# A hybrid decoder block: the order of the quarter products in the input projection, the queue of its stores, and single extra matmuls

## Chip, core and metric

The kernel runs on one core of one Trainium2 chip. The time is the device time of one execution in microseconds (us), lower is better; the time before is the median of three runs.

## What is computed

One decoder layer in fp32, with 512 tokens (S), a model width of 2048 (D), 8 heads of 128, and an MLP of 8192. Cut to what matters:

```
h = rmsnorm(x, g_mix);  z = h @ w_in          # 2048 columns in, 10248 out
cb, cc, cv, q, k, v, f, gate_c, gate_a = split(z)
conv   = (cb * causal_conv3(cc * cv)) @ w_conv_out
attn   = softmax(q k^T / sqrt(128) + decay(f), causal) v @ w_attn_out
x      = x + (sigmoid(gate_c + b) * conv + sigmoid(gate_a + b) * attn) @ w_mix_out
h = rmsnorm(x, g_mlp);  x = x + (relu(h @ w_ff1) ** 2) @ w_ff2
out = rmsnorm(x, g_final)
```

The first product is called the input projection, h @ w_ff1 is ff1.

## The kernel before

Each large fp32 operand is split into a high and a low part (`split`, L99: ScalarE copies the high part, L100, VectorE subtracts it from the source, L101), and three matmuls, high x high, high x low and low x high, replace one. In `mm_cols` (L126) a weight quarter of 8 tiles stands still and the tokens move, 256 columns at a time: L139 and L141 are the matmuls with the high part, 32 in a run, L143 the 16 with the low part. `mm_rows` (L145; L156, L157 and L159) exchanges the two operands, for the attention values.

The input projection and ff1 save one product in eight by a scheme of seven products (a form of Strassen's), written as a `Group` (L168). A group covers a pair of column blocks and all tokens. Its weights are four quarters X00, X10, X01, X11, each a load of about 1 MB through SP's queue (`load`, L177, the DMA at L183) into one of four buffers x0 to x3, which a list named `free` hands out in the order in which `done` (L219) gives them back. A `run` (L189) splits one quarter, or a difference of quarters, into one of two buffers `th` and `tl`, and makes 48 matmuls with one of seven prepared token matrices: A11, A12, A22, S1, S2, S3, S4 (`Quarters`, L336, for the input projection, `Blocks`, L694, for ff1).

- `head` (L222) loads X00 and X10, runs A11 into bank a and A12 into bank b; their sum is the quarter (0,0) of the output.
- `tail` (L238) loads X01 and X11 and makes the runs S4 (bank c), S2 (bank a, on top of A11), S3 (bank d), S1 (bank a again) and A22 (bank d again). Its operands are X11, then X01 - X00, X11 - X01 and X11 - (X01 - X00) by three subtractions of VectorE ahead of S2 (`sub`, L103, the instruction at L104), and one more for A22. `snap` (L197, the copy at L200) takes a bank into an output buffer of ScalarE's, `plus` (L207) adds a bank to one by VectorE, and `put` stores the quarter. There are five output buffers (`otile`, L70).

In the input projection five groups, gV0 and four of keys and queries, are begun by their heads while the token matrices of the differences are being made (L462), and their tails follow (L466). gV0 and the key groups' quarters are not kept in between, so their tails load all four again, in the order X00, X10, X01, X11. Then come, each with head and tail together (`whole`, L457), the second value group gV1, six conv groups (L591), with attention (`attend`, L529) interleaved in the first four and the convolution (`conv_job`, L566) after, and eight groups of the gates (L606). ff1 has sixteen groups: the heads of the first two are begun together, then their tails, then the rest (L917 to the loop after it). Their `put` squares the quarters and forms sums of them in a buffer r, which GpSimd's queue stores (L852, L853).

The results of the projection go to HBM and are read again: keys, queries and values (L437, L444), conv inputs (L595), gates (L611), attention outputs (L563) and conv outputs (L579). All these stores stand in SP's queue, between the loads. GpSimd's queue holds, in this part of the kernel, memsets for attention's masks and two columns of `u` in each convolution (L571), which wait for a free buffer.

Nobody writes an order between engines by hand: the framework sorts each engine's instructions by its own model of the time, with the program's order as priority, and puts the waits.

`apart` (L581) gives some groups two extra matmuls in the run of S4, ahead of the third and the sixth of its eight tiles: 256 columns each, into a bank named spare that nobody reads. They are given to one conv group, to every third group of the gates and to every fourth of ff1. The PSUM banks p0 to p7 are laid out in the order in which the program first names them.

Of the kernel before, what the change touches and what calls it, by code (L numbers as in the profile page):

```python
# [15 lines left out]
P = 128  # L16
# [4 lines left out]
HS = S // 2  # L21
# [8 lines left out]
COL_K, COL_Q = 3 * CW + AW, 3 * CW  # L30
# [15 lines left out]
def tile_hybrid_block(ctx: ExitStack, tc, x, g_mix, w_in, b_f, b_gate, conv_w, w_conv_out,  # L46
# [74 lines left out]
    parts([P, 4, S])  # L121
    for i in range(7):
        pair(i, F32, "lay")


    def mm_cols(ps, Sx, hi, lo, first, extra=None):  # L126


        ps = ps[0].rearrange("p (j s) -> p j s", j=2)
        nq = hi.shape[1]  # L130
        for part in range(2):
            for q in range(nq):
                Sh, Sl = Sx(q)
                if extra and part == 0:
                    extra(q, Sh, hi[:, q, :])
                for j in range(2):
                    o, js = ps[:, j, :], slice(j * P, (j + 1) * P)
                    if part == 0:
                        nc.tensor.matmul(o, hi[:, q, js], Sh, start=first and q == 0 and j == 0, stop=False,  # L139
                                         skip_group_check=True)  # L140
                        nc.tensor.matmul(o, hi[:, q, js], Sl, start=False, stop=False, skip_group_check=True)  # L141
                    else:
                        nc.tensor.matmul(o, lo[:, q, js], Sh, start=False, stop=q == nq - 1, skip_group_check=True)  # L143
# [24 lines left out]
    class Group:  # L168
# [53 lines left out]
        def head(self, keep=False, between=lambda: None):  # L222
# [12 lines left out]
                self.done(1, 0)  # L235
            self.put(0, 0, s1)

        def tail(self):  # L238
            if self.at:
                X = self.X  # L240
            else:
                X = {(i, 0): self.load(i, 0) for i in range(2)}
            X[0, 1], X[1, 1] = self.load(0, 1), self.load(1, 1)
            a = self.a
            c = self.acc("c")
            self.run(c, "S4", X[1, 1], True)
# [12 lines left out]
            d1 = self.snap(d, self.scale)  # L259
            self.run(a, "S1", X[0, 0], False)  # L260
            self.done(0, 0)
            s4 = self.snap(a, self.scale)
            add(d1, d1, s4)
            self.put(1, 1, d1)
            self.plus(s4, c, self.scale)
            self.put(0, 1, s4)
            self.run(d, "A22", X[1, 0], False)
            self.done(1, 0)
            self.plus(s2, d)
            self.put(1, 0, s2)  # L270
# [162 lines left out]
    def store_v(c0, w):  # L433
        def put(i, j, v):
            c = c0 + j * w
            n = min(w, AW - c)
            nc.sync.dma_start(out=v_d[2 * i:2 * i + 2, :, c:c + n].rearrange("t p c -> p t c"), in_=v[:, :, :n])  # L437
            if n < w:
                add(fl[:, 2 * i:2 * i + 2, :], v[:, :, n:], bf.unsqueeze(1).to_broadcast([P, 2, NH]))
        return put  # L440

    def store_kq(hp):
        def put(i, j, v):
            nc.sync.dma_start(out=kq_d[j, 2 * hp:2 * hp + 2, :, i * HS:(i + 1) * HS].rearrange("b p c -> p b c"), in_=v)  # L444
        return put

    cV = COL_AV + AW // 2
# [1 line left out]
    gV0 = Group(w_in, COL_AV, COL_AV + VW, VW, Q1.moving, mm_rows, ((4,), (3,), (6,), (7,)), store_v(0, VW))  # L449

    def kq(hp, banks):
        return Group(w_in, COL_K + hp * HS, COL_Q + hp * HS, HS, Q1.moving, mm_cols, banks, store_kq(hp), QSCALE)

    def steady(n):
        return ((2 + n % 2,), (3 - n % 2,), (0,), (1,))

    def whole(g):  # L457
        g.head(True)
        g.tail()

    heads = [gV0] + [kq(hp, ((a,), (3,), (6,), (7,))) for hp, a in enumerate((0, 1, 2, 5))]
    for g in heads:  # L462
# [1 line left out]
    Q1.sums()  # L464
    ph.close()
    for g in heads:  # L466
        g.tail()
    whole(gV1)

    ph = ExitStack()  # L470
# [58 lines left out]
    def attend(h):  # L529
        kT, qT = at("kT"), at("qT")  # L530
        nc.sync.dma_start(out=kT, in_=kq_d[0, h])
        nc.sync.dma_start(out=qT, in_=kq_d[1, h])
        vv = at("vv", [P, NT, P])
        nc.sync.dma_start(out=vv, in_=v_d[:, :, h * P:(h + 1) * P].rearrange("t p c -> p t c"))
        o = bank(4, "o")
        for qi in range(NT):
            n = (qi + 1) * P
            qs = slice(qi * P, n)
            sc = bank(5 + 2 * (qi % 2), "sc")
            nc.tensor.matmul(sc[:, :n], qT[:, qs], kT[:, :n], start=True, stop=False)  # L540
# [12 lines left out]
            nc.vector.tensor_scalar(out=p[:, :n], in0=p[:, :n], scalar1=rs, scalar2=None, op0=ALU.mult)  # L553
            tp = bank(6, "tp")
            for ki in range(qi + 1):
                nc.tensor.transpose(tp[:, ki * P:(ki + 1) * P], p[:, ki * P:(ki + 1) * P], ident)
            pt = at("pt")
            nc.vector.tensor_copy(pt[:, :n], tp[:, :n])
            for ki in range(qi + 1):
                nc.tensor.matmul(o[:, qs], vv[:, ki, :], pt[:, ki * P:(ki + 1) * P], start=(ki == 0), stop=(ki == qi))  # L560
        ov = at("ov")
        nc.scalar.activation(out=ov, in_=o, func=AF.Copy)
        nc.sync.dma_start(out=a_d[h], in_=ov)  # L563


    def conv_job(f):  # L566
        cv, cc, cb = at("cv"), at("cc"), at("cb")
        for k, t in enumerate((cb, cc, cv)):
            nc.sync.dma_start(out=t, in_=z_d[k, f])
        u = at("u", [P, S + 2])  # L570
        nc.gpsimd.memset(u[:, 0:2], 0.0)  # L571
        nc.vector.tensor_tensor(out=u[:, 2:], in0=cv, in1=cc, op=ALU.mult)
        w = [cwT[:, i * CT + f:i * CT + f + 1] for i in range(3)]
        y = at("y")
        nc.vector.tensor_scalar(out=y, in0=u[:, 0:S], scalar1=w[0], scalar2=None, op0=ALU.mult)
        for i in (1, 2):
            nc.vector.scalar_tensor_tensor(out=y, in0=u[:, i:S + i], scalar=w[i], in1=y, op0=ALU.mult, op1=ALU.add)
        nc.vector.tensor_tensor(out=y, in0=cb, in1=y, op=ALU.mult)
        nc.sync.dma_start(out=y_d[f], in_=y)  # L579

    def apart(i):  # L581


        spare = bank(i, "spare")

        def extra(q, Sh, h):
            if q in (2, 5):
                nc.tensor.matmul(spare[:, :HS], Sh[:, :P], Sh if q == 2 else h, start=True, stop=True)
        return {"S4": extra}

    n = 0  # L591
    for g in (4, 2, 0, 5, 3, 1):
        def put_z(i, j, v, g=g):
            f = 4 * (g % 2) + 2 * j
            nc.sync.dma_start(out=z_d[g // 2, f:f + 2, :, i * HS:(i + 1) * HS].rearrange("b p c -> p b c"), in_=v)  # L595
# [10 lines left out]
    for f in range(0, KT, 2):  # L606
        def put_g(i, j, v, f=f):
            for b in range(2):
                k = j * KT + f + b
                nc.scalar.activation(out=v[:, b, :], in_=v[:, b, :], func=AF.Sigmoid, bias=bgT[:, k:k + 1])  # L610
            nc.sync.dma_start(out=g_d[j, f:f + 2, :, i * HS:(i + 1) * HS].rearrange("b p c -> p b c"), in_=v)  # L611
# [259 lines left out]

    def ff1(g, banks):
        return Group(w_ff1, g * S, g * S + HS, HS, Q2.moving, mm_cols, banks, put_u(g),
                     extra=apart(0) if g % 4 == 2 else {})

    ph.close()
    ph = ExitStack()
# [246 lines left out]
```

## Time and profile before

| | before |
|---|---|
| median of 3 runs | 2484.23 us (2478.97 to 2494.47) |
| the profiled execution's own time | 2487.1 us |
| span of the profile, first to last instruction | 2485.4 us |
| mean granted TensorE clock | 0.996 |
| matmuls | 16911 |
| read from HBM, written to it | 370.26 MB, 92.27 MB |

In a profile PE is TensorE's matmuls, PEld its weight loads, DVE is VectorE, ACT ScalarE, POOL GpSimd, SP the engine that only issues DMAs. Matmuls are pipelined: one of 256 columns lasts 279 ns on the page, but the next starts some 113 ns after it. A row of a timeline gives start, length, engine, line and tiles, a count where equal instructions are merged, and in brackets the idle time before it with what ended that. In a row of the waits stand who waited for whom, the total in us, how often, and the longest.

### The profile page before, as it was taken

Reading aid. Unit: us, or ns where it says so; the run is one execution under the profiler, and the core shown is the slowest. Engines: PE = TensorE matmul, PEld = TensorE weight load, DVE = VectorE, ACT = ScalarE, POOL = GpSimd, SP = SyncE. Lnnn points to the kernel's source line nnn. Section 1 sums busy time; section 2 is a strip of 40 time slices with the busy share of each in tenths; the row PEclk is TensorE's granted clock in tenths of the full one; section 3 lists DMA queues with packets and bytes.
Section 4 is the critical chain, followed back from the end, with each engine's and each line's share of the span. In section 5 each row is a group of like instructions: output and inputs, shape, how many; then the busy total and the mean of one; then the engine's idle time right before and its main releaser. Section 6 shows DMA issues by size and latency. Waiting matters only on the chain.

```text
span 2485.4 us, 39120 instructions
## 1 busy us (share of the span) xinstructions
PE 2438.5 (98%) x16911; PEld 2251.6 (91%) x16911; DVE 1911.5 (77%) x1575; ACT 1149.5 (46%) x1144; POOL 111.9 (5%) x184
## 2 busy tenths in 40 slices
PE   7999999999999999999999999999999999999997
PEld 7999989999999988888899999999998888888886
DVE  7877676788776844425688988988987888889897
ACT  5333434334445532225555666666665333333334
POOL 0000000000000000000000000000011001100000
PEclk9999999999999999999999999999999999999999
DMA  7555444456534454335646556556487576655662
GB/s 238 170 164 164 137 140 152 149 159 223 169 118 150 161 191 139 129 136 195 200 161 208 210 202 225 184 202 240 172 301 274 179 253 217 240 192 185 233 228 94
DMA packets 290496, 465.07 MB, mean 187 GB/s; under 512 B 10300, under 2 KB 194708, under 8 KB 290196
## 3 DMA queue, kind: packets, MB, share of 16 engines
q1 hardware_dynamic: 261280, 330.40, 41.0%
q0 software_dynamic: 28176, 131.08, 14.1%
q8 instruction: 132, 2.16, 0.4%
q10 hardware_dynamic: 868, 1.10, 0.1%
q14 instruction: 40, 0.33, 0.0%
HBM read 370.26 MB, written 92.27 MB: 186 GB/s over the span
## 4 chain that ended last, share of the span: by engine, by line
PE 70%; DVE 5%; DMA 3%; issue 2%; ACT 1%; SPq 0%; DVEq 0%; POOLq 0%; POOL 0%; ACTq 0%
PE a L139 5%; PE a L141 5%; PE a L143 5%; PE a L156 4%; PE a L157 4%; PE a L159 4%; PE d L141 3%; PE d L139 3%; PE d L143 3%; PE pt L301 2%; PE pn L310 2%; PE pt L303 2%; PE pn L309 2%; PE pn L308 2%; PE pt L302 2%; PE d L156 2%
## 5 line engine op out<-in xcount | busy, mean ns | idle before, releaser
L101 DVE TENSOR_TENSOR tl<-x,th 128x2048 fp32r<-128x2048 f32 (+1 forms) x252 | 574.8, 2288 | 211.9 <-ACT th L100 195.1
L100 ACT ACTIVATE th<-x 128x2048 fp32r<-128x2048 f32 (+1 forms) x252 | 482.7, 1918 | 493.4 <-PE a L141 180.4
L104 DVE TENSOR_TENSOR x<-x,x 128x2048 f32<-128x2048 f32 (+1 forms) x144 | 329.2, 2286 | 13.5 <-DMA x<-in_w_in_dram 7.9
L100 ACT ACTIVATE th<-y 128x2048 fp32r<-128x2048 f32 x80 | 153.8, 1923 | 219.9 <-PE a L157 134.6
L101 DVE TENSOR_TENSOR tl<-raw,th 128x2048 fp32r<-128x2048 f32 x40 | 91.7, 2293 | 152.0 <-ACT th L100 151.4
L156 PE MATMUL a<-th,us 128*128 128x512 f32 x512 | 200.2, 391 | 2.3 <-ACT o L861 2.3
L157 PE MATMUL a<-th,us 128*128 128x512 f32 x512 | 200.1, 391 | 0.0
L101 DVE TENSOR_TENSOR tl<-y,th 128x2048 fp32r<-128x2048 f32 x80 | 182.9, 2288 | 19.4 <-ACT th L100 19.1
L139 PE MATMUL a<-ST,th 128*128 128x256 f32 x768 | 180.0, 279 | 6.7 <-ACT th L100 6.7
L141 PE MATMUL a<-ST,th 128*128 128x256 f32 x768 | 179.5, 279 | 0.0
L100 ACT ACTIVATE th<-raw 128x2048 fp32r<-128x2048 f32 x40 | 76.8, 1919 | 175.5 <-PE pt L302 71.5
L139 PEld LDWEIGHTS a<-ST,th 128*128 128x128 f32 x768 | 146.4, 191 | 7.4 <-ACT th L100 7.3
L141 PEld LDWEIGHTS a<-ST,th 128*128 128x128 f32 x768 | 146.3, 191 | 0.0
L139 PE MATMUL a<-S,th 128*128 128x256 f32 x576 | 134.4, 279 | 5.5 <-ACT th L100 5.5
L159 PE MATMUL a<-tl,us 128*128 128x512 f32 x512 | 136.8, 389 | 0.0
L141 PE MATMUL a<-S,th 128*128 128x256 f32 x576 | 133.7, 277 | 0.0
L100 ACT ACTIVATE th<-t 128x2048 fp32r<-128x2048 f32 x32 | 61.4, 1919 | 132.1 <-DVE t L104 77.4
L139 PE MATMUL d<-ST,th 128*128 128x256 f32 x512 | 117.7, 276 | 0.0
L141 PE MATMUL d<-ST,th 128*128 128x256 f32 x512 | 117.7, 276 | 0.0
L156 PEld LDWEIGHTS a<-th,us 128*128 128x128 f32 x512 | 96.5, 189 | 22.6 <-ACT o L861 2.5
L157 PEld LDWEIGHTS a<-th,us 128*128 128x128 f32 x512 | 96.6, 189 | 20.1
L139 PEld LDWEIGHTS a<-S,th 128*128 128x128 f32 x576 | 108.2, 188 | 7.0 <-ACT th L100 6.7
(283 smaller groups left out, 6273.2 us busy)
## 6 DMA issues: line engine op xcount, KB each, us to landing
x<-in_w_in_dram SPq DMA_DIRECT2D x86, 1024.0 KB, 5.8
x<-in_w_ff_dram SPq DMA_DIRECT2D x66, 1024.0 KB, 8.0
y<-in_w_ff_dram SPq DMA_DIRECT2D x64, 1024.0 KB, 7.6
us<-s_d POOLq DMA_DIRECT2D x48, 1024.0 KB, 9.2
s_d<-rh POOLq DMA_DIRECT2D x32, 896.0 KB, 5.1
s_d<-r POOLq DMA_DIRECT2D x32, 896.0 KB, 5.5
raw<-in_w_mix_out_dram SPq DMA_DIRECT2D x24, 1024.0 KB, 5.1
g_d<-o SPq DMA_DIRECT2D x32, 256.0 KB, 2.2
```

The lines of the kernel that those rows point to most:

```text
L100: nc.scalar.activation(out=hi, in_=src, func=AF.Copy)
L101: nc.vector.tensor_tensor(out=lo, in0=src, in1=hi.bitcast(F32), op=ALU.subtract)
L104: nc.vector.tensor_tensor(out=out, in0=a, in1=b, op=ALU.subtract)
L139: nc.tensor.matmul(o, hi[:, q, js], Sh, start=first and q == 0 and j == 0, stop=False, skip_group_check=True)
L141: nc.tensor.matmul(o, hi[:, q, js], Sl, start=False, stop=False, skip_group_check=True)
L143: nc.tensor.matmul(o, lo[:, q, js], Sh, start=False, stop=q == nq - 1, skip_group_check=True)
L156: nc.tensor.matmul(o, Sh, hi[:, q, :], start=begin and q == 0, stop=False, skip_group_check=True)
L157: nc.tensor.matmul(o, Sl, hi[:, q, :], start=False, stop=False, skip_group_check=True)
L159: nc.tensor.matmul(o, Sh, lo[:, q, :], start=False, stop=q == nq - 1, skip_group_check=True)
L301: nc.tensor.matmul(ps[j], hi[:, q, js], xh, start=k == 0, stop=False)
L302: nc.tensor.matmul(ps[j], hi[:, q, js], xl, start=False, stop=False)
L303: nc.tensor.matmul(ps[j], lo[:, q, js], xh, start=False, stop=k == kt - 1)
```

## The change

It has four parts.

1. The groups of the input projection get a new tail, `tail2`, with the runs in the order S1 (bank c), S3 (d), S2 (a), S4 (c, on top of S1), A22 (d, on top of S3), one subtraction ahead of each of S1, S3, S2 and A22. Its loads come in the order X01, X00, X11, X10, as far as the head has not kept them. ff1 keeps the old tail, but with the loads in the order X11, X01, X00, X10.
2. The stores of keys, queries, values, conv inputs, gates, attention and conv outputs go from SP's queue to GpSimd's.
3. The eight PSUM banks are named once at the start, p0 to p7.
4. The pairs of extra matmuls become single ones of 192 columns, ahead of the fifth tile of S4, with that tile's own weights and tokens, in one conv group and every third group of the gates, as before, and in every third group of ff1 (2, 5, 8, 11, 14). The four key groups and the first two groups of ff1 get another in the run of S3: its first matmul is made once more on 192 columns into bank d just ahead, and overwritten.

The diff, cut:

```diff
+    for i in range(8):
+        bank(i, "lay")
...
     def mm_cols(ps, Sx, hi, lo, first, extra=None):
...
-                if extra and part == 0:
+                if extra == "first" and part == 0 and q == 0:
+                    nc.tensor.matmul(ps[:, 0, :192], hi[:, q, :P], Sh[:, :192], start=True, stop=False,
+                                     skip_group_check=True)
+                elif extra and extra != "first" and part == 0:
                     extra(q, Sh, hi[:, q, :])
...
+        def quarters(self, *order):
+            X = self.X if self.at else {}
+            for ij in order:
+                if ij not in self.at:
+                    X[ij] = self.load(*ij)
+            return X
+
         def tail(self):
-            if self.at:
-                X = self.X
-            else:
-                X = {(i, 0): self.load(i, 0) for i in range(2)}
-            X[0, 1], X[1, 1] = self.load(0, 1), self.load(1, 1)
+            X = self.quarters((1, 1), (0, 1), (0, 0), (1, 0))
...
+        def tail2(self):
+            X = self.quarters((0, 1), (0, 0), (1, 1), (1, 0))
+            a = self.a
+            sub(X[0, 0], X[0, 1], X[0, 0])
+            c = self.acc("c")
+            self.run(c, "S1", X[0, 0], True)
+            sub(X[0, 1], X[1, 1], X[0, 1])
+            d = self.acc("d")
+            self.run(d, "S3", X[0, 1], True)
+            sub(X[0, 1], X[1, 1], X[0, 0])
+            self.done(0, 0)
+            d1 = self.snap(d, self.scale)
+            self.plus(d1, c, self.scale)
+            self.run(a, "S2", X[0, 1], False)
+            sub(X[1, 0], X[1, 0], X[0, 1])
+            self.done(0, 1)
+            s2 = self.snap(a)
+            self.plus(d1, a, self.scale)
+            self.put(1, 1, d1)
+            self.run(c, "S4", X[1, 1], False)
+            self.done(1, 1)
+            s4 = self.snap(c, self.scale)
+            self.plus(s4, a, self.scale)
+            self.put(0, 1, s4)
+            self.run(d, "A22", X[1, 0], False)
+            self.done(1, 0)
+            self.plus(s2, d)
+            self.put(1, 0, s2)
...
-            nc.sync.dma_start(out=v_d[...], in_=v[:, :, :n])        # likewise kq_d, a_d, y_d, z_d, g_d
+            nc.gpsimd.dma_start(out=v_d[...], in_=v[:, :, :n])
...
         return Group(w_in, COL_K + hp * HS, COL_Q + hp * HS, HS, Q1.moving, mm_cols, banks, store_kq(hp), QSCALE,
+                     extra={"S3": "first"})
...
         def extra(q, Sh, h):
-            if q in (2, 5):
-                nc.tensor.matmul(spare[:, :HS], Sh[:, :P], Sh if q == 2 else h, start=True, stop=True)
+            if q == 4:
+                nc.tensor.matmul(spare[:, :192], h[:, :P], Sh[:, :192], start=True, stop=True)
...
     def ff1(g, banks):
-                     extra=apart(0) if g % 4 == 2 else {})
+                     extra={"S3": "first"} if g < 2 else apart(0) if g % 3 == 2 else {})
```

The calls of `tail` in the input projection (in `whole` and after the five heads) become calls of `tail2`.

More of the change, by code (lines that the diff above doesn't have):

```diff
@@ L436, in put @@
             n = min(w, AW - c)
-            nc.sync.dma_start(out=v_d[2 * i:2 * i + 2, :, c:c + n].rearrange("t p c -> p t c"), in_=v[:, :, :n])
+            nc.gpsimd.dma_start(out=v_d[2 * i:2 * i + 2, :, c:c + n].rearrange("t p c -> p t c"), in_=v[:, :, :n])
             if n < w:
@@ L443, in put @@
         def put(i, j, v):
-            nc.sync.dma_start(out=kq_d[j, 2 * hp:2 * hp + 2, :, i * HS:(i + 1) * HS].rearrange("b p c -> p b c"), in_=v)
+            nc.gpsimd.dma_start(out=kq_d[j, 2 * hp:2 * hp + 2, :, i * HS:(i + 1) * HS].rearrange("b p c -> p b c"), in_=v)
         return put
@@ L451, in kq @@
     def kq(hp, banks):
-        return Group(w_in, COL_K + hp * HS, COL_Q + hp * HS, HS, Q1.moving, mm_cols, banks, store_kq(hp), QSCALE)
+        return Group(w_in, COL_K + hp * HS, COL_Q + hp * HS, HS, Q1.moving, mm_cols, banks, store_kq(hp), QSCALE,
+                     extra={"S3": "first"})
     def steady(n):
@@ L458, in whole @@
         g.head(True)
-        g.tail()
+        g.tail2()
     heads = [gV0] + [kq(hp, ((a,), (3,), (6,), (7,))) for hp, a in enumerate((0, 1, 2, 5))]
@@ L466, in tile_hybrid_block @@
     for g in heads:
-        g.tail()
+        g.tail2()
     whole(gV1)
@@ L562, in attend @@
         nc.scalar.activation(out=ov, in_=o, func=AF.Copy)
-        nc.sync.dma_start(out=a_d[h], in_=ov)
+        nc.gpsimd.dma_start(out=a_d[h], in_=ov)
     def conv_job(f):
@@ L578, in conv_job @@
         nc.vector.tensor_tensor(out=y, in0=cb, in1=y, op=ALU.mult)
-        nc.sync.dma_start(out=y_d[f], in_=y)
+        nc.gpsimd.dma_start(out=y_d[f], in_=y)
     def apart(i):
@@ L594, in put_z @@
             f = 4 * (g % 2) + 2 * j
-            nc.sync.dma_start(out=z_d[g // 2, f:f + 2, :, i * HS:(i + 1) * HS].rearrange("b p c -> p b c"), in_=v)
+            nc.gpsimd.dma_start(out=z_d[g // 2, f:f + 2, :, i * HS:(i + 1) * HS].rearrange("b p c -> p b c"), in_=v)
         if n < NH // 2:
@@ L610, in put_g @@
                 nc.scalar.activation(out=v[:, b, :], in_=v[:, b, :], func=AF.Sigmoid, bias=bgT[:, k:k + 1])
-            nc.sync.dma_start(out=g_d[j, f:f + 2, :, i * HS:(i + 1) * HS].rearrange("b p c -> p b c"), in_=v)
+            nc.gpsimd.dma_start(out=g_d[j, f:f + 2, :, i * HS:(i + 1) * HS].rearrange("b p c -> p b c"), in_=v)
         whole(Group(w_in, COL_GC + f * P, COL_GA + f * P, HS, Q1.moving, mm_cols, steady(n), put_g,
```

## Prediction

> **What bounds the kernel now.** I read the page first, then the busy time by stage, then TensorE's waits in the stages that the change touches, then the chain of waits and the timelines round the longest of them.
>
> ```profile
> span 2485.4 us, 39120 instructions
> PE 2438.5 (98%) x16911; PEld 2251.6 (91%) x16911; DVE 1911.5 (77%) x1575; ACT 1149.5 (46%) x1144; POOL 111.9 (5%) x184
> ```
> ```profile
> core 0: us, PE busy (x) PEld busy (x) DVE busy (x) ACT busy (x) POOL busy (x), PEclk, DMA share, GB/s
> 88.00:232.50 144.50, 138.85 (x1200) 137.46 (x1199) 109.78 (x59) 57.01 (x41) 0.00 (x0) 1.00 0.55 172
> 273.00:494.50 221.50, 217.28 (x1725) 201.32 (x1724) 161.47 (x234) 89.96 (x122) 0.11 (x1) 1.00 0.45 141
> 494.50:878.80 384.30, 382.86 (x3370) 382.28 (x3370) 302.90 (x205) 187.62 (x188) 0.70 (x7) 1.00 0.52 164
> 1233.40:1345.00 111.60, 104.32 (x873) 103.28 (x872) 90.81 (x73) 62.19 (x68) 5.60 (x9) 0.97 0.49 164
> 1345.00:1858.00 513.00, 512.95 (x4524) 512.75 (x4522) 447.25 (x332) 322.40 (x323) 33.32 (x60) 1.00 0.61 216
> ```
>
> TensorE is busy for 98% of the span. The stretches are, in order, the tails of the five groups begun together, attention with the first conv groups, the other conv groups and the gate groups, the start of ff1, and the rest of ff1. Idle in them are 5.7, 4.2, 1.4, 7.3 and 0.05 us (length less PE busy); beyond that only the pace of the matmuls could win anything. TensorE's waits in the stretches 88 to 233, 494 to 879 and 1233 to 1858 are:
>
> ```profile
> PE a L139 <- ACT th L100: 4.4, 4, 1.9
> PE a L156 <- ACT th L100: 0.8, 1, 0.8
> ...
> PE a L139 <- ACT th L100: 1.1, 2, 0.6
> ...
> PE a L139 <- ACT th L100: 6.7, 3, 2.6
> PE c L139 <- ACT th L100: 0.5, 1, 0.5
> ```
>
> Nearly all of it stands before a run into bank a, that is before S2, the second run of the old tail.
>
> **Order of the tail and of its loads.** The timelines of VectorE, ScalarE and TensorE at the first of those waits:
>
> ```profile
> 120.33 4.61 DVE L104 TENSOR_TENSOR x<-x,x 128x2048 f32<-128x2048 f32 x2
> ...
> 122.73 1.91 ACT L100 ACTIVATE th<-x 128x2048 fp32r<-128x2048 f32 x1 [5.72 <-DVE x L104]
> ...
> 124.69 0.39 PE L139 MATMUL a<-S,th 128*128 128x256 f32 x1 [1.92 <-ACT th L100]
> ```
>
> ScalarE had been idle for 5.72 us for the subtractions. S2 needs three of them in a row (4.61 / 2 = 2.3 us each, so 6.9) and a 1.9 us split: 8.8 us behind the loads, and the run of S4 that should cover them is shorter, as these starts of neighbouring runs show:
>
> ```profile
> 130.25 0.28 PE L139 MATMUL d<-S,th 128*128 128x256 f32 x1
> 135.69 0.28 PE L139 MATMUL a<-S,th 128*128 128x256 f32 x1
> ...
> 187.61 0.28 PE L139 MATMUL d<-S,th 128*128 128x256 f32 x1
> 193.27 0.28 PE L139 MATMUL a<-S,th 128*128 128x256 f32 x1
> ```
>
> A run of 48 matmuls takes 5.44 us (113 ns each) in the first pair of rows, 5.66 (118 ns) in the second: the same instructions with two paces, 0.22 us apart a run. I come back to that. In the order S1, S3, S2, S4, A22 each of S1, S3 and S2 needs one further subtraction, S4 none, A22 one, which has a run's time to spare: 2.3 + 1.9 = 4.2 us against 5.44. S1 needs two loads instead of the four that S4 waited for in the grouped heads. So the waits of the first stretch go: its 5.7 us, and four times 0.1 for the restart, since the first matmul behind a wait takes 0.39 us and not 0.28 (124.69 against 130.25): 6.1 us. The stretch at 118 ns that 187.61 lies in began behind one of those waits and lasted five runs, 1.1 us; I count half, 0.5. Sum 6.6. In the conv and gate groups 1.1 and two restarts: 1.3.
>
> ff1 keeps the old order but loads X11 first. What its first three groups wait for is in the chain of waits, with VectorE and TensorE beside it:
>
> ```profile
> 1279.26 5.74 DMA x<-in_w_ff_dram
> ...
> 1293.75 1.92 ACT th L100
> ...
> 1313.21 8.71 DMA s_d<-r
> ...
> 1291.38 2.28 DVE L104 TENSOR_TENSOR x<-x,x 128x2048 f32<-128x2048 f32 x1
> ...
> 1295.72 0.38 PE L139 MATMUL a<-ST,th 128*128 128x256 f32 x1 [2.64 <-ACT th L100]
> ...
> 1297.20 0.41 PE L139 MATMUL a<-ST,th 128*128 128x256 f32 x1
> ...
> 1300.61 0.29 PE L139 MATMUL a<-ST,th 128*128 128x256 f32 x1
> ...
> 1338.48 0.58 PE L139 MATMUL a<-ST,th 128*128 128x256 f32 x1 [2.46 <-ACT th L100]
> ...
> 1341.61 0.28 PE L139 MATMUL a<-ST,th 128*128 128x256 f32 x1
> ```
>
> The load at 1279.26 is the fourth of group 1's tail, X11, which S4 reads first and on which the third subtraction (1291.38) hangs. As the first of four it comes in a slot that is free two or three runs earlier, so groups 0 and 1 lose their waits. Behind the 2.64 us wait TensorE ran at half pace: 16 matmuls from 1297.20 to 1300.61, 3.41 us instead of 16 x 0.113 = 1.81, 1.6 lost (PEclk of the stretch 0.97). Group 2 lost 2.46 and, on 14 matmuls in 3.13 us, 1.5 more; but its chain goes through the store of r (8.71 us), which the change leaves alone, so I count half. Groups 0 and 1: (6.7 - 2.46) + 0.5 + 1.6 = 6.3; group 2: 2.0. Sum 8.3 us.
>
> The Trainium skill (TensorE: Matmul & The Clock Gate, HAM oscillation — how this bites in real kernels) has the array fall to half clock for idle gaps above about 3.4 us. The trace disagrees: 2.64 us were enough. By that rule the half pace would have another cause and stay, and the sum would be 1.6 + 0.8 = 2.4 us smaller.
>
> **More work for VectorE.** The new tail combines out of PSUM three times where it added once from SBUF: one more pass a group.
>
> ```profile
> L107 DVE TENSOR_TENSOR o<-c,o 128x512 f32<-128x512 f32 x31 | 21.2, 684 | 0.1
> ```
>
> 0.7 us in 20 groups, 14 in all. VectorE is busy 110 of 144 us and 303 of 384 in these stages, so TensorE's run covers it: 0. Bank c must be read for d1 between the end of S3 and S4's first write, one run of S2 (5.44 us): the copy of d, S4's low split (2.3) and this pass take about 3.6. If VectorE's queue held another 2.3 us subtraction ahead, the cover would be used up.
>
> **Stores in GpSimd's queue.** All loads stay in SP's, with no store ahead that waits for data. Landing, and GpSimd's own waits:
>
> ```profile
> g_d<-o SPq DMA_DIRECT2D x32, 256.0 KB, 2.2
> s_d<-r POOLq DMA_DIRECT2D x32, 896.0 KB, 5.5
> ...
> POOL u L571 <- DVE y L577: 121.8, 7, 46.8
> ```
>
> A store through GpSimd lands between 2.2 us (as SP's, nearest in size) and 5.5 later than its issue. It holds one of five output buffers, of which a group (38 us) takes four, and attention reads keys and queries a whole group (gV1) after they were written: 0. In its queue stores now stand among the memsets of u, which wait up to 46.8 us; that is a rival. GpSimd is busy for 5%.
>
> The Trainium skill (DMA: Bandwidth & Descriptors, Issuing engine by pattern) gives plain stores to the Sync engine. By its fit for GpSimd's path (Anatomy of one DMA) 256 KB take an estimated 2.0 + 0.6 = 2.6 us; no store of this size goes that way here, and the sum stays the same by either.
>
> **Banks in natural order.** The program's banks land at other addresses; the same matmul shows no difference between them:
>
> ```profile
> L139 PE MATMUL c<-S,th 128*128 128x256 f32 x288 | 67.6, 278 | 0.2 <-ACT th L100 0.2
> L139 PE MATMUL a<-A,th 128*128 128x256 f32 x288 | 67.1, 278 | 0.0
> ```
>
> 0 either way, as nothing hangs on the bank but who must have read it.
>
> **Extra matmuls.** They compute nothing that is used. Pairs of 256 columns are replaced by single ones of 192, in other places. What a pair does, and one of the pair alone:
>
> ```profile
> 505.44 0.28 PE L139 MATMUL c<-S,th 128*128 128x256 f32 x1
> ...
> 511.20 0.28 PE L139 MATMUL a<-S,th 128*128 128x256 f32 x1
> ...
> 1291.10 1.98 PE L143 MATMUL c<-ST,tl 128*128 128x256 f32 x16
> ...
> 1332.44 0.28 PE L588 MATMUL spare<-th,ST 128*128 128x256 f32 x1
> ...
> 1333.97 2.05 PE L143 MATMUL c<-ST,tl 128*128 128x256 f32 x16
> ```
>
> A run with a pair takes 5.76 us, 0.32 over: two slots and a dozen matmuls at 118 ns. The single one at 1332.44 left the stream at the slower pace (2.05 us for 16 matmuls, 1.98 otherwise). So an extra matmul can switch the pace, in either direction, and it then holds. Seven pairs at 0.32 and one taken apart at 0.4 cost 2.6 us now; 15 single ones at a slot (0.113 at most, two thirds of it by columns) cost at most 1.7: 0.9 won. What one of 192 does to the pace no row shows. Its bounds are all of the touched stages at 113 (about 3 us better) and at 118 (43 worse, below). I take 0: unlike the old ones it reads the very weights and columns of the matmul behind it, so the stream's operands keep their order.
>
> **Sum.** 6.6 + 1.3 + 8.3 + 0.9 = 17.1 us off the profiled execution's 2487.1: 2470. That execution is 2.9 above the median of the runs, 2484.23; on the median's scale the forecast is 2467, 0.7% less. Attention's stretch is left at 0: its four groups interleave with small matmuls, and the 4.2 us of idle time there bound what a better order could win; I allow as much to be lost.
>
> **Rivals.**
> - *The waits close up elsewhere.* VectorE at 76 to 87% in these stages just runs late at another run. For it: the chain in ff1 goes through VectorE's and ScalarE's work on r as well. Only the loads' part is won, half of the 14.9 in the first and third stage: 2467 + 7 + 5 for new short waits, about 2480.
> - *More goes than I count*: also group 2's other 2.0, the heads' stretch at 118 ns wholly (0.5), attention's 4.2 and a few us of paces there: 8 to 12 us, 2457.
> - *Each lone extra flips the pace.* For it: the row at 1332.44. The conv and gate groups would be slow between the first and second and between the third and fourth extra, six groups x 7 x 0.22 = 9.2; ff1 in some 8.4 groups, 13: 2467 + 22 = 2489.
> - *Every extra leaves the stream at 118 ns* (the other side). Then 19 runs of the heads, (878.8 - 505.4) / 5.44 = 68 runs of the conv and gate groups and some 107 of ff1 take 0.22 more: 43 us, 2510, 1.0% slower. Against it: the old pairs brought the pace back. It decides slower from about 190 of these 194 runs on.
> - *The extras do nothing, a store sticks.* A store behind a memset of u that waits 46.8 us holds buffers beyond a group's 38 us: 9 us, 2476.
>
> **How the numbers follow.** Forecast 0.47 (own range 2459 to 2478), waits close up 0.15, more goes 0.14, flips 0.11, all slow 0.08, store sticks 0.05. Faster by over 1% (about what a measurement of this kernel can tell from no change) means below 2459.4: two thirds of "more goes" and a little of the forecast, 0.13. Slower by over 1% means above 2509.1: most of "all slow" and a rest of "flips", 0.08. Within 1%: 0.79. The range 2454 to 2497 leaves out "all slow", the lower end of "more goes" and the upper of "flips", under 0.2.
>
> **What would show it.** Right: no wait of TensorE above 0.5 us between 88 and 233 and in ff1's groups 0 and 1, no half pace there, runs of 5.44 us behind each extra. Wrong: 16 low matmuls in 2.05 us behind an extra of 192 columns; a wait of TensorE before S4 (bank c); x loads that issue no earlier; a ScalarE copy into an output buffer that waits for a store.

## The result, and the profile after

After the change the kernel takes 2514.66 us (median of 4 runs, 2509.77 to 2517.93), beside 2484.74 us (4 runs) before: a ratio of 1.0115, 95% interval 1.0078 to 1.0151. It is 1.2% slower; the forecast was 2467 us, and its range ended at 2497. The profiled execution took 2513.57 us. The head of its page:

```profile
span 2511.8 us, 39247 instructions
PE 2447.4 (97%) x16910; PEld 2259.6 (90%) x16910; DVE 1923.0 (77%) x1597; ACT 1147.5 (46%) x1144; POOL 178.1 (7%) x280
```

The span grew by 26.4 us and TensorE's busy time by 9: most of what was lost is idle time of TensorE. The windows after, with bounds at the same work as the five windows of before:

```profile
core 0: us, PE busy (x) PEld busy (x) DVE busy (x) ACT busy (x) POOL busy (x), PEclk, DMA share, GB/s
83.80:221.60 137.80, 137.80 (x1207) 137.80 (x1206) 112.17 (x66) 55.54 (x41) 10.88 (x15) 1.00 0.60 182
262.00:481.90 219.90, 217.50 (x1727) 201.45 (x1726) 162.92 (x239) 88.04 (x120) 16.25 (x26) 1.00 0.45 140
481.90:864.10 382.20, 381.54 (x3366) 381.34 (x3365) 306.65 (x210) 187.99 (x190) 34.09 (x54) 1.00 0.53 166
1218.70:1331.20 112.50, 104.63 (x878) 103.83 (x877) 91.08 (x74) 63.76 (x69) 5.92 (x10) 0.97 0.49 164
1331.20:1886.70 555.50, 526.55 (x4519) 523.99 (x4518) 447.72 (x332) 321.60 (x322) 33.42 (x61) 0.98 0.57 199
```

Row by row against before: the heads' tails are 6.7 us shorter and have no idle time left; attention is 1.6 and the conv and gate groups are 2.1 shorter; the start of ff1 is 0.9 longer; the rest of ff1 is 42.5 us longer, with 29 us idle where there were 0.05, and the granted clock fell from 1.00 to 0.98. So all of the loss lies in ff1, the stage to which the forecast had given its largest gain, and nearly all in the groups of it to which the forecast had given nothing.

In stages from the first matmul of each to that of the next (worked out from the starts of TensorE's instructions, us):

```
                               before   after
before the first tail            87.7    83.8
five tails                      144.8   137.8
group gV1                        40.4    40.4
four conv groups, attention     221.7   219.9
other conv groups and gates     384.3   382.3
conv, attention, mix products   354.6   354.5
ff1                             626.8   668.0
ff2 to the end                  625.2   625.1
```

The first row isn't the change: in the experiments below it lies between 83 and 89 us. ff1 alone is +41.2; the rest sums to about -15, of which 3.9 stand in the first row. Group by group of ff1, by the same starts (the last group up to the end of its runs):

```
                  groups 0 and 1    group 2    groups 3 to 15, each
before                  85.8          42.6         38.1 to 38.4
after                   85.3          43.6         39.6 to 44.1
```

38.1 us are seven runs of 5.44. Before, every group from group 3 on ran without a break; after, none did. The waits of TensorE and of VectorE for loads, within 1218 to 1887 us of the changed kernel:

```profile
DVE x L104 <- DMA x<-in_w_ff_dram: 50.0, 16, 5.0
...
PE a L144 <- ACT th L100: 36.2, 15, 3.8
```

TensorE waits 15 times in front of bank a's second run, which is S2, once in every group but group 1; before it was 6.7 us in three places. VectorE waits about as often for a load, 50 us in all, in a subtraction (L104). What joins the two is the chain of waits around group 3 (columns: start, length, what):

```profile
1337.09 2.30 DVE tl L101
1339.41 8.66 DMA x<-in_w_ff_dram
...
1348.16 0.10 DVE x L104
...
1350.37 0.69 DVE o L107
...
1359.60 1.94 DVE r L890
1361.53 2.21 DVE x L104
...
1363.83 1.92 ACT th L100
...
1365.79 0.39 PE a L144
```

Read it from the top: the low split of group 2's last run frees a buffer; the load that waited for it takes 8.66 us; VectorE starts a subtraction as it lands; then VectorE is the chain for 15 us, up to the subtraction S2 needs; split; S2. VectorE's timeline at that place, after:

```profile
1342.53 2.29 DVE L101 TENSOR_TENSOR tl<-x,th 128x2048 fp32r<-128x2048 f32 x1 [3.15 <-ACT th L100]
1344.74 0.68 DVE L107 TENSOR_TENSOR o<-o 128x512 f32<-128x512 f32 x1
1348.16 2.29 DVE L104 TENSOR_TENSOR x<-x,x 128x2048 f32<-128x2048 f32 x1 [2.74 <-DMA x<-in_w_ff_dram]
1350.37 0.69 DVE L107 TENSOR_TENSOR o<-c,o 128x512 f32<-128x512 f32 x1
...
1361.45 2.28 DVE L104 TENSOR_TENSOR x<-x,x 128x2048 f32<-128x2048 f32 x1
```

and at the same place of a group before, with ScalarE's split of S2's operand last:

```profile
1432.85 2.29 DVE L101 TENSOR_TENSOR tl<-x,th 128x2048 fp32r<-128x2048 f32 x1 [3.14 <-ACT th L100]
1435.06 0.69 DVE L107 TENSOR_TENSOR o<-o 128x512 f32<-128x512 f32 x1
1435.66 2.29 DVE L104 TENSOR_TENSOR x<-x,x 128x2048 f32<-128x2048 f32 x1
1437.86 0.68 DVE L107 TENSOR_TENSOR o<-c,o 128x512 f32<-128x512 f32 x1
...
1448.94 2.29 DVE L104 TENSOR_TENSOR x<-x,x 128x2048 f32<-128x2048 f32 x1
...
1451.32 1.93 ACT L100 ACTIVATE th<-x 128x2048 fp32r<-128x2048 f32 x1 [4.64 <-DVE x L104]
```

The passes are the same ones in the same order. From the last low split to the third subtraction VectorE needs 16.1 us before (1432.85 to 1448.94) and 18.9 after (1342.53 to 1361.45): the difference is, to 0.1 us, the 2.74 us that it stands in front of X00 = X01 - X00. Group 3, like every later one, still has X00 and X10 from its head, so of the new order X11, X01, X00, X10 only X11, X01 is left, the reverse of before. The load that gets the last free buffer is now X01, and VectorE's first subtraction needs it; before, it was X11, which only the second one needs. Before, S2's split ended at 1453.25 and S2 began at 1454.27: 1.0 us in hand. 2.74 against 1.0 leaves 1.7 us of waiting, and 1365.79 does stand behind a wait of 1.68. The same sum comes out in all thirteen groups from 3 to 15: VectorE waits for the load for 2.3 to 4.7 us, and TensorE's wait in front of S2 is 0.9 to 1.2 us shorter each time.

### The profile page after: what moved, and what is told of

Read it like the earlier page. It is cut to its first block, busy times and chain, and to the rows that moved or that the text cites. A ratio compares the mean times of both kernels' runs of the same rounds, so it can differ in the third digit from the quotient of the medians.

```text
span 2511.8 us, 39247 instructions
## 1 busy us (share of the span) xinstructions
PE 2447.4 (97%) x16910; PEld 2259.6 (90%) x16910; DVE 1923.0 (77%) x1597; ACT 1147.5 (46%) x1144; POOL 178.1 (7%) x280
## 3 DMA queue, kind: packets, MB, share of 16 engines
q1 hardware_dynamic: 237216, 305.23, 38.2%
## 4 chain that ended last, share of the span: by engine, by line
PE 59%; DVE 9%; DMA 6%; issue 3%; ACT 3%; DVEq 0%; POOLq 0%; POOL 0%; ACTq 0%; SPq 0%
DMA x<-in_w_ff_dram 6%; PE a L164 4%; PE a L161 4%; PE a L162 4%; DVE tl L101 4%; PE a L144 3%; PE a L146 3%; PE a L148 3%; PE d L146 3%; PE d L144 3%; ACT th L100 2%; PE pt L342 2%; PE pn L349 2%; PE pn L350 2%; PE pn L348 2%
## 5 line engine op out<-in xcount | busy, mean ns | idle before, releaser
L104 DVE TENSOR_TENSOR x<-x,x 128x2048 f32<-128x2048 f32 (+1 forms) x144 | 329.3, 2287 | 57.6 <-DMA x<-in_w_ff_dram 50.0
L144 PE MATMUL a<-ST,th 128*128 128x256 f32 x768 | 191.8, 291 | 36.2 <-ACT th L100 36.2
L146 PE MATMUL a<-ST,th 128*128 128x256 f32 x768 | 189.7, 289 | 0.0
L144 PEld LDWEIGHTS a<-ST,th 128*128 128x128 f32 x768 | 154.1, 201 | 39.2 <-ACT th L100 39.2
L146 PEld LDWEIGHTS a<-ST,th 128*128 128x128 f32 x768 | 154.0, 201 | 0.0
L144 PE MATMUL c<-S,th 128*128 128x256 f32 x576 | 134.6, 278 | 0.7 <-DVE o L107 0.7
L146 PE MATMUL c<-S,th 128*128 128x256 f32 x576 | 134.3, 278 | 0.0
L164 PEld LDWEIGHTS a<-tl,us 128*128 128x128 f32 x512 | 96.0, 188 | 20.1 <-DVE tl L101 0.2
```

Source lines behind the costliest of these rows:

```text
L104: nc.vector.tensor_tensor(out=out, in0=a, in1=b, op=ALU.subtract)
L164: nc.tensor.matmul(o, Sh, lo[:, q, :], start=False, stop=q == nq - 1, skip_group_check=True)
```

## The experiments

The theory: the reversed loads in ff1's steady groups (3 to 15) are the whole loss, and all else in the change is worth a gain. The rivals: the new tail, the stores in GpSimd's queue, the extras or the banks cost something in ff1, too, or the loads are harmless without them. Experiments that start from the changed kernel have its line numbers, but for a line or two. Each ratio is to the kernel before, measured again beside the experiment (medians of 2489 to 2492 us).

**The old order of loads in ff1.**

```diff
         def tail(self):
-            X = self.quarters((1, 1), (0, 1), (0, 0), (1, 0))
+            X = self.quarters((0, 0), (1, 0), (0, 1), (1, 1))
```

> The changed kernel with the loads of ff1's tail back in the old order (X00, X10, X01, X11); all else as changed. Theory (load order: X01, which all three subtractions ahead of S2 need, is now the last of the four loads, and VectorE waits for it): the stretch of ff1 goes back from 668 to about 625 us and the kernel to 2470, some 14 us under before. Rival (the other extra matmuls in ff1 cost it, by the pace or otherwise): ff1 stays near 668 and the kernel at 2515.

Measured: 2476.68 us, ratio 0.9951 (0.9936 to 0.9965). Its waits in front of S2:

```profile
PE a L144 <- ACT th L100: 7.2, 3, 2.9
```

One line turns 1.2% slower into 0.5% faster. ff1 takes 632.9 us in the profile, 35 less than in the changed kernel and 6 more than before. These 6 aren't waits: the profiled execution was the slowest of six (2482.89 us), and 2011 of its matmuls in ff1 start 118 ns after the one ahead where there were 276 before, some 8 us at 4.5 ns each. Of this pace more below.

**The new order alone.** The kernel before, with `quarters` and the changed order in ff1's tails, and nothing else of the change:

```diff
-        def tail(self):
+        def tail(self, new=False):
...
+            X = self.quarters(*(((1, 1), (0, 1), (0, 0), (1, 0)) if new else ((0, 0), (1, 0), (0, 1), (1, 1))))
```

> The kernel before with one edit, the new load order (X11 first, X01 behind it) in ff1's tails. Theory (load order): ff1 takes about 41 us more, the kernel 2525, 1.6% slower than before. Rival (extra matmuls or the stores' queue): no change, 2485.

Measured: 2527.54 us, ratio 1.0157 (1.0135 to 1.0178), ff1 666.6 us. The waits (here with the line numbers of before):

```profile
PE a L139 <- ACT th L100: 28.2, 14, 3.4
```

So the order of two loads is enough by itself, and taking it away removes the waits: the theory holds from both sides. The ratios differ by 2% between these two kernels and by 0.4% between the second and the changed one; that 0.4% (1.0157 against 1.0115, intervals that just overlap) is what the rest of the change gives back.

**The new order only where the head has kept nothing.**

```diff
-            X = self.quarters((1, 1), (0, 1), (0, 0), (1, 0))
+            X = self.quarters(*(((0, 1), (1, 1)) if self.at else ((1, 1), (0, 1), (0, 0), (1, 0))))
```

Only group 1 has kept nothing, so it alone loads X11 first; group 0 and groups 2 to 15 load X01, then X11, as before. Where the expectations below speak of the first two groups, it is group 1 alone.

> The changed kernel with the new load order in ff1's first two groups alone, whose tails load all four quarters; the other fourteen load X01 before X11 as before. My prediction's step (the new order helps the first two groups by 6 us): 4 to 6 us under the kernel with the old order throughout, about 2465. Theory (X01 late is bad anywhere): group 0 loses about 4 us and the kernel lies at 2473 or more.

Measured: 2473.73 us, ratio 0.9934 (0.9914 to 0.9955). ff1 takes 623.9 us, 2.9 less than before. But the gain isn't where it was sought: groups 0 and 1 take 85.8 us, exactly as before, and group 2 takes 38.2 instead of 42.6. Against the first experiment, where group 1 alone differs, group 2 gains 5.2 us (43.4) and groups 0 and 1 0.2 (86.1). In all seven kernels with this order group 2 takes 38.2 to 40.6 us; why it is group 2 that gains was not taken apart. The medians, 2473.7 and 2476.7, have intervals that overlap. This kernel is the base of most of the following ones.

**ff1 on the new tail as well** (`tail2`, with the previous group's sums of r made behind S2, as in `tail`):

```diff
             s2 = self.snap(a)
+            while later:
+                later.pop(0)()
...
     for g in heads:
-        g.tail()
+        g.tail2()
```

> The changed kernel with ff1 on the new tail too (S1, S3, S2, S4, A22, loads X01, X00, X11, X10), the deferred squaring work taken up behind S2's copy. Theory (one subtraction ahead of each run, X01 no longer last): no wait before any run of ff1, 621 us for it, the kernel at 2460 to 2468. Rival (VectorE at 87% has no room for one more pass a group): waits of TensorE for VectorE or ScalarE remain, 2475 or more.

Measured: 2541.88 us, ratio 1.0211 (1.0194 to 1.0228); ff1 683.0. The order that served the input projection is the worst of all here. Its waits:

```profile
ACT r L875 <- DMA s_d<-r: 69.1, 15, 6.2
...
PE a L144 <- ACT th L100: 16.5, 16, 1.7
...
PE b L148 <- DVE tl L101: 14.3, 8, 1.9
...
PE b L144 <- ACT th L100: 8.2, 6, 6.2
```

The first row led to a new theory: r has one buffer, its two sums now follow each other by one run, and the store takes 7.1 us here (5.5 before). So the sums were moved behind S1, two runs earlier:

```diff
             self.run(c, "S1", X[0, 0], True)
+            while later:
+                later.pop(0)()
```

> The kernel with ff1 on the new tail took 2541.9 us (span 2538.3, ff1 683.0), with the sums of the group before made behind S2; there ScalarE waits 69 us for the stores of the one buffer r (15 waits), since the two sums of r follow each other by one run of 5.4 us, and a store of r takes 5.5. Here those sums are made behind S1, two runs earlier. Theory: the one buffer r is the cause: ScalarE's wait for its store goes below 15 us in total, ff1 falls to 625 to 650 us, the time to 2475 to 2505. Rival: VectorE and ScalarE have no room for the sums anywhere in this order, since every run but S4 has a subtraction in front of its split: the waits move to S3 and S2, and the time stays above 2520 us.

Measured: 2523.86 us, ratio 1.0142 (1.0121 to 1.0164); ff1 660.3, and ff2 639.0 where it had been 633.2 with the sums behind S2, and 625 before.

```profile
ACT r L875 <- DMA s_d<-r: 46.6, 15, 5.2
...
PE a L144 <- ACT th L100: 11.8, 9, 2.2
...
PE b L148 <- DVE tl L101: 10.0, 8, 1.7
```

The theory of the buffer falls as a whole cause: the wait for it shrank by a third, to 47 us and not to 15, and the time stayed above 2520, as the rival said. That VectorE and ScalarE have no room for the sums in this order fits, but only argued: what holds ff1 on this tail was not taken apart further.

**The input projection back on the old tail**, from the kernel with 2473.7 us:

```diff
-        g.tail2()
+        g.tail(((0, 0), (1, 0), (0, 1), (1, 1)))
```

> The kernel with the new load order in ff1's first two groups only (2473.7 us, span 2471.7), with the input projection back on the old tail (order S4, S2, S3, S1, A22, loads X00, X10, X01, X11); stores, banks and extras stay new. Theory: the new order is what takes the waits before S2 out of the heads' stretch (181.7 us against 189.8 in the profile of before) and about 1 us out of the conv and gate groups: 2474 + 8 + 1 = 2483 us, TensorE's waits for ScalarE's split before S2 back in every grouped tail. Rival: the extras and the stores in GpSimd's queue did part of it, then 2474 + 4 = 2478 us or less, and the waits are not all back.

Measured: 2490.18 us, ratio 1.0003 (0.9989 to 1.0017). Windows of the 25 runs of the five tails, first with the new tail, then with the old one:

```profile
87.60:225.40 137.80, 137.80 (x1207) 137.80 (x1206) 112.42 (x66) 55.53 (x41) 10.89 (x15) 1.00 0.60 182
```

```profile
86.30:231.70 145.40, 139.70 (x1206) 138.49 (x1205) 110.50 (x60) 56.91 (x41) 10.15 (x14) 1.00 0.54 171
```

The new tail is worth all that the other kernel gained, 16 us by the medians. In the profiles it is 7.7 in the five tails, 2.2 in the conv groups with attention and 6.6 in the other conv groups and the gates (388.8 against 382.3 us). The heads came out as the theory said. The 6.6 us came unexpected: TensorE's waits in them are 2.1 us, and 768 starts at 118 ns instead of 17, at 4.5 ns each, another 3.4.

**The stores back in SyncE's queue**, from the same kernel: the six `nc.gpsimd.dma_start` of v_d, kq_d, a_d, y_d, z_d and g_d become `nc.sync.dma_start`.

> The kernel with the new load order in ff1's first two groups only (2473.7 us), with the stores of the input projection, of attention and of the gates back in SyncE's queue. Theory: the buffers cover either landing time and no load waits long enough behind a store to matter: no change, 2474 us within 3. Rival: in the new order a store that waits for its group's end stands ahead of the next group's loads in SyncE's queue; a load that issues later than its slot is free brings back a wait of 1 to 2 us before S1 or S3 in some of the 17 groups: 2480 to 2495 us.

Measured: 2470.27 us, ratio 0.9928 (0.9906 to 0.9949). No store delayed a load enough to matter, and GpSimd's queue brought nothing. A store of a gate quarter lands, first with the change (GpSimd), then here:

```profile
g_d<-o POOLq DMA_DIRECT2D x32, 256.0 KB, 2.8
```

```profile
g_d<-o SPq DMA_DIRECT2D x32, 256.0 KB, 2.5
```

**Without the lines that lay out the banks**:

```diff
-    for i in range(8):
-        bank(i, "lay")
```

> The kernel with the new load order in ff1's first two groups only (2473.7 us), without the lines that lay out the banks in natural order. Theory: the bank's address has no price: 2474 us within 3, stage by stage the same. Rival: accumulating into one bank while another one next to it is read costs something; then matmuls of the same tiles show another mean, and the time is over 3 us off on either side.

Measured: 2473.75 us, ratio 0.9940 (0.9920 to 0.9960), stage by stage the same within 0.5 us except ff1 (627.0). The bank's address has no price that shows.

**Without any extra matmul**: `extra={}` for all groups, so that nothing but the computation is left.

> The kernel with the new load order in ff1's first two groups only (2473.7 us), without any extra matmul (they compute nothing that is used). Theory: in a stream at 113 ns an extra costs its slot, 15 x 0.085 to 0.113 us = 1.3 to 1.7 us, and only twice was one seen to stand where a stream at 118 ns went back to 113; without them 2474 - 1.5 + a few us = 2472 to 2480 us. Rival: the extras are what keeps the streams at 113 ns; without them the groups of conv and gates and of ff1 fall to 118 ns for good: up to (68 + 107) runs x 0.22 = 38 us, 2495 to 2512 us. Second rival: they never did anything, 2472 us.

Measured: 2493.45 us (2479.58 to 2503.09), ratio 1.0012 (0.9988 to 1.0037). Fifteen matmuls that compute nothing are worth 20 us by the medians; leaving them out cost more than the new tail had won. The eleven runs without them spread widely, but each is slower than every run with them (2468.68 to 2475.05); the profiled one, at 2501.74, is one of five above 2501. The same window of ff1, without them and with them:

```profile
1340.00:1850.00 510.00, 510.00 (x4333) 510.00 (x4332) 433.16 (x325) 311.39 (x311) 29.04 (x54) 1.00 0.58 201
```

```profile
1340.00:1850.00 510.00, 509.07 (x4447) 508.03 (x4447) 444.18 (x332) 320.75 (x323) 33.71 (x60) 1.00 0.61 214
```

Both are busy from end to end at a granted clock of 1.00; one makes 4333 matmuls, 118 ns each, the other 4447. What an extra does stands in the kernel with them, around the one of group 11:

```profile
1668.03 0.28 PE L144 MATMUL c<-ST,th 128*128 128x256 f32 x1
1668.15 0.28 PE L146 MATMUL c<-ST,th 128*128 128x256 f32 x1
1668.27 0.25 PE L628 MATMUL spare<-ST,th 128*128 128x192 f32 x1
1668.35 0.31 PE L144 MATMUL c<-ST,th 128*128 128x256 f32 x1
...
1669.09 0.28 PE L144 MATMUL c<-ST,th 128*128 128x256 f32 x1
1669.20 0.28 PE L146 MATMUL c<-ST,th 128*128 128x256 f32 x1
1669.31 0.28 PE L144 MATMUL c<-ST,th 128*128 128x256 f32 x1
```

Ahead of it starts are 0.12 us apart, from 1669.09 on 0.11: the stream had been at 118 ns since two late starts in group 9 (0.28 and 0.23 us behind the one ahead), and goes on at 113 for the next 1008 matmuls.

**The extras of before** (pairs of 256 columns, in eight groups, none in the key groups and ff1's first two):

> The kernel with the new load order in ff1's first two groups only (2473.7 us, span 2471.7), with the extra matmuls as before the change: pairs of 256 columns in one conv group, three gate groups and ff1's groups 2, 6, 10, 14, none in the key groups and ff1's first two. Without any extra the kernel took 2493 us: its streams behind a wait stay at 118 ns for up to 4559 matmuls. Theory: an extra, of either kind, brings a stream at 118 ns back to 113 within some five matmuls, and what counts is how many matmuls stand between a wait and the next extra. Fewer places (8 instead of 15) and two slots instead of one: 7 x 0.32 - 15 x 0.1 = +0.7, and up to 1008 x 0.0045 = 4.5 us more wherever a slow stretch goes on longer: 2474 to 2485 us. Rival: only the ones of 192 columns, with the weights of the matmul behind them, hold the pace: 2490 us or more.

Measured: 2474.59 us, ratio 0.9941 (0.9921 to 0.9962). By the time of the kernel either kind does: what matters is that there are some. But one of these pairs is taken apart, and its second matmul, alone, left a fast stream at 118 ns for 1350 matmuls here, about 6 us.

**An extra in every group** behind attention and in ff1, with the stores in SyncE's queue:

> The kernel with the new load order in ff1's first two groups only and the stores in SyncE's queue (2470.3 us, span 2465.8), with a single extra of 192 columns in every conv and gate group behind attention and in every group of ff1 from the third on (30 instead of 15 in all). Theory: each extra bounds a slow stretch to one group's 336 matmuls (1.5 us at 4.5 ns each) at a price of 0.09 to 0.11 us: 15 x 0.1 = +1.5, and minus what slow stretches are left, 0 to 6 us a run: 2466 to 2472 us, with less spread. Rival: an extra can also throw a fast stream to 118 ns, and with 30 of them some will: 2475 us or more.

Measured: 2478.43 us, ratio 0.9952 (0.9938 to 0.9967). The time is the rival's, but not the cause: no row shows an extra that threw a fast stream out. ff1 took 630.9 us where it had been 621.4 in the kernel with the stores in SyncE's queue. TensorE's waits in it hardly grew (9.1 us, from 7.7), but 1098 starts are at 118 ns instead of 66, most of them in three stretches of some 300 matmuls that each begin behind a wait of 0.2 to 1.7 us and end at the next extra. Whether that is more than the chance of one execution isn't settled.

The best two, 2470.3 us (stores in SyncE's queue) and 2473.7, can't be told apart: 0.9928 and 0.9934, intervals of 0.004. Both beat the kernel before by 0.7% and the changed one by about 1.8%.

## Why the prediction was wrong, point by point

The step that failed is "ff1 keeps the old order but loads X11 first ... = 6.3; group 2: 2.0. Sum 8.3 us". It priced the new order of loads where the profile of before showed waits, in three groups, and left out the thirteen others, where it showed none. But the diff changes the order there as well. As two of the four quarters are kept, loading X11 earlier makes X01 the last, and VectorE needs X01 first. The number that was needed stood in the trace of before: 1.0 us in hand between S2's split and S2. What was measured:

- Groups 3 to 15: forecast 0, measured +43 us (539 after, 496 before). All of ff1, +41.2: 36.7 us of waits where there were 7.2, less 2.3 in front of ff2's first matmul that are gone, make 27.2; half pace, nine windows of 3.41 us where there had been two, 11.3; slower starts behind the waits and other small things the remaining 2.7.
- Groups 0 and 1: forecast -6.3, measured -0.5, since group 0 has kept its two quarters as well, and its wait in front of S2 grew from 1.6 to 3.5 us while group 1's of 2.6 went. Group 2: forecast -2.0, measured +1.0. Where group 1 alone loads X11 first, groups 0 and 1 gain nothing and group 2 gains 4.4: the waits of the first two groups weren't the loads' alone, and the wait of group 2, put down half to the store of r, went with them (42.6 and 43.4 us in the two kernels with the old order throughout).

The other terms and the rivals:

- Heads' stretch: forecast -6.6, measured -7.0, and no wait of TensorE above 0.5 us there, as "what would show it" asked. Where the old tail is put back, the waits are back (4.5 us in front of S2).
- Conv and gate groups: forecast -1.3, measured -2.0 in the changed kernel. By the reverse experiment the old tail costs 6.6 there, half of it a pace that was lost behind its waits.
- VectorE's extra pass: forecast 0. One of the signs of being wrong did come, a wait of TensorE in front of S4 (bank c, 509.89) for that pass, once and 0.7 us long, in a conv group where the convolution's passes stand in VectorE's queue, too.
- GpSimd's stores, the banks: forecast 0 each, nothing measured. The rival of a store stuck behind a memset of u, and the Trainium skill's preference for the Sync engine's queue (DMA: Bandwidth & Descriptors, Issuing engine by pattern), made no difference that can be measured; the estimate of 2.6 us for such a store by the same page stands beside the 2.8 of the row.
- Extras: forecast -0.9 by counting slots. The sign was beside the point: what they are worth is the pace, and without them 20 us are lost. For the extras of 192 columns "each lone extra flips the pace" and "every extra leaves the stream at 118 ns" both fell.
- The rival that came nearest by its number, all slow at 2510, was wrong in its cause; that it lies within 5 us of the result is luck. "The waits close up elsewhere" came nearest in kind, a wait that returns at another place, but it put that down to VectorE's own load of work, not to a transfer at the head of its queue, and priced the new waits at 5 us where groups 3 to 15 lost 43.

## What to carry to other kernels

When a diff reorders loads, go through every loop that calls the changed line, above all the iterations in which the profile shows no wait, and ask for each which transfer is now the last and what stands in its consumer's queue behind it: an engine that works in order passes its wait on to all that follows. A stage without idle time is no stage without a price: look up the margin (here 1.0 us) before costing an edit at nothing. And before you count a seemingly idle instruction by its slot, leave it out once and look at the pace of what follows.

## What the runs showed of the hardware

- *Two paces, and what moves between them.* The 256-column matmuls of a stream start 113 or 118 ns apart, at the same granted clock. These counts are from the thirteen profiled executions of this case, in the five tails, the conv and gate groups behind attention, and ff1. In 420 stretches without an extra and without a start later than 126 ns after the one ahead the pace never changed. Behind a wait of over 0.2 us, a fast stream went on slow 30 times and fast 87; a slow one became fast 31 times and stayed 11. A single extra of 192 columns into the spare bank left a slow stream fast 13 times of 14, within some seven matmuls, and a fast one fast all 82 times. The other form, the run's first matmul made twice, restored only 12 of 22. The lone second half of a pair, of 256 columns, left a fast stream slow in all three kernels that have it. Slow starts by kernel: 8209 without extras, 1128 with them (2473.7 us), 359 with the stores in SyncE's queue (2470.3 us), at 4.5 ns each. Why there are two paces no run shows.
- *Half pace.* It is a granted clock of 0.50 (213 ns a start instead of 113) for a window of 3.41 us, and by the granted clock in the traces these windows lie on a fixed grid: within a run they begin whole multiples of 3.413 us apart (in the changed kernel at 1252.23, 1323.91, 1491.17 and 1532.13, which is 21, 49 and 12 windows on). What decides is TensorE's idle time within one window of that grid, not the length of a wait. In all thirteen profiles, each of the 56 windows at full clock that a slow one followed held 1.79 us of idle time or more; none of the 232 with 0.3 to 1.79 us was followed by one, and 6 with 1.83 to 1.94 weren't either. Two waits of the changed kernel (the brackets), and two windows of the grid around each:

```profile
1407.02 0.39 PE L144 MATMUL a<-ST,th 128*128 128x256 f32 x1 [2.87 <-ACT th L100]
...
1698.09 0.39 PE L144 MATMUL a<-ST,th 128*128 128x256 f32 x1 [2.46 <-ACT th L100]
```

```profile
core 0: us, PE busy (x) PEld busy (x) DVE busy (x) ACT busy (x) POOL busy (x), PEclk, DMA share, GB/s
1402.42:1405.83 3.41, 1.73 (x16) 1.53 (x14) 3.41 (x4) 0.77 (x1) 0.53 (x1) 1.00 0.95 389
1405.83:1409.25 3.42, 2.23 (x19) 2.23 (x20) 3.42 (x2) 3.42 (x3) 0.00 (x0) 1.00 0.17 67
1695.97:1699.38 3.41, 1.29 (x11) 1.29 (x12) 3.41 (x4) 3.25 (x4) 0.00 (x0) 1.00 0.42 168
1699.38:1702.79 3.41, 3.41 (x19) 3.41 (x18) 3.38 (x6) 2.63 (x4) 0.00 (x0) 0.50 0.22 54
```

The wait of 2.87 us is cut by the grid into 1.68 and 1.19 us of idle time (length less PE busy), and the clock stays at 1.00; of the shorter one, 2.46 us, 2.12 fall into one window, and the next is granted 0.50. The Trainium skill's bound of about 3.4 us (TensorE: Matmul & The Clock Gate, HAM oscillation — how this bites in real kernels) is too high for this kernel, where 2.46 us were enough. Half pace makes a wait of 2 us dearer than it looks: 16 matmuls at 100 ns more are another 1.6 us.
